# Another order of the work at the boundaries between matrix products: ScalarE norms the first token tile, and the second one's transposes stand inside the third one's tail

## The chip, the cores and the metric

The kernel runs on one core of a Trainium2 chip. The core has a matrix engine (TensorE, PE in the profile), three engines for elementwise work (VectorE or DVE, ScalarE or ACT, GpSimd or POOL), and SyncE (SP), which issues most of the transfers here. Each engine works through its own instructions in order; semaphores make one wait for another. The metric is the device time of one execution in microseconds (us), as a median of runs.

## The reference

One inference step of a backbone with two layers, width 1024, over 384 tokens: 128 of a context pass and 256 latent ones. Both groups use the same weights, but are modulated by different vectors. Everything is float32. Per layer:

```python
def trunk_layer(x, mod, lp, cache):
    sh1, sc1, g1, sh2, sc2, g2 = jnp.split(mod, 6, axis=-1)
    h = rmsnorm(x, lp['g_norm'][0]) * (1.0 + sc1) + sh1
    m, ctx_tensors = token_mixer(h, lp, cache)
    x = x + g1 * rmsnorm(m, lp['g_norm'][1])
    h = rmsnorm(x, lp['g_norm'][2]) * (1.0 + sc2) + sh2
    f = jnp.square(jax.nn.relu(h @ lp['w_mlp1'])) @ lp['w_mlp2']
    x = x + g2 * rmsnorm(f, lp['g_norm'][3])
    return x, ctx_tensors
```

`token_mixer` projects h with `w_in`, runs four branches (retention, S5, gated linear attention, neighbourhood attention), gates their outputs and multiplies the sum by `w_out`. `mod` is a product of `silu(c)` with the weight `w_ada`.

## The kernel before

A product of two float32 matrices is made of three products of parts: each operand is split into a high part (cast to fp32r) and a low part (the rest), and TensorE adds high x high, high x low and low x high in PSUM (the lines L209, L210 and L211 of the profile, in this order). The activations' parts are `hh` and `hl`. The weights come as raw tiles `wf` of 128 x 1024 by DMA; ScalarE casts one to its high part `wh` (L144), VectorE subtracts for the low part `wl` (L156). `prefetch(n)` does this until n weights are ready. Most split weights lie in tiles called `wh` and `wl`, some in spare rows (`rC`, `rB`) or in a spare pair called `r`.

The tokens are three tiles of 128: tile 0 is the context, tiles 1 and 2 are latent. Two kinds of product alternate. In one (`gemm_rows`, `rows`) the tokens are on the output's partitions: a weight row of 128 x 1024 is added into six accumulators of 128 x 512, two a tile. In the other (`gemm_a`, `up`) the output's channels are on the partitions, 128 x 384 each, 24 matmuls.

A layer's residual and norm need whole rows of the accumulators, and the next product needs the normed activations transposed. The function `boundary` orders the work at that place. It is called four times: behind `w_out` in layer 0 (boundary 1, whose tile 1 is transposed at 480.81 us in the trace), behind the MLP of layer 0 (boundary 2, at 775.62), behind `w_out` in layer 1 (boundary 3, at 1210.64), and at the end, with no norm. Inside it the code's order is each engine's order:

- `tail(i, half)`: the last five weight rows, 15 matmuls of 512 columns, for one half of token tile i.
- `residual(i)`, a generator that runs up to its next `yield` at each `next`: ScalarE squares the accumulator (L783), VectorE multiplies it by the gain (L786), VectorE and GpSimd make the reciprocal root (`rstd`, L684 and L685), VectorE updates x (L789), ScalarE squares the new x (L791), a second rstd, and `m` = x times rstd: one half on ScalarE (L797), one on VectorE (L798).
- `normed(i)`: eight transposes of `m` on TensorE (L770) into two PSUM tiles of four channel blocks each. The first four blocks: multiply by the scale and add the shift on VectorE (L812, L813), cast to `hh` on ScalarE (L814). The other four: four calls of 128 columns on ScalarE (L817), the cast on VectorE (L819). VectorE makes both low parts (L818, L820).
- `split`: the first four column blocks ("banks" here) of the next product, each eight matmul triples deep. Over tokens 0 to 255 (tiles 0 and 1) first, 96 matmuls of 256 columns, and then, when tile 2 is normed, over tokens 256 to 383, 96 of 128 columns.

After boundaries 1 and 3, which stand ahead of an MLP, the program goes on with `up(4)`, then in turns one weight row of the second MLP product and one more `up`. Beside it runs a background job, `ada`, for the next modulation vectors: SyncE loads a row block of `w_ada` into a tile `r` (L581), and VectorE multiplies it twice (L583). The tiles `r` come from the same three buffers as the spare weights of the split, so such a load waits until the matmuls that read the spare weight are done.

## Time and profile before

| | |
|---|---|
| median of 3 runs | 1502.18 us (1501.23 to 1503.28) |
| the profiled execution | 1499.83 us, its span 1498.1 us, mean granted clock 0.968 |
| TensorE (PE) | 1418.7 us busy, 95% of the span |
| weight loads (PEld) | 1258.7 us, 84%, beside the matmuls |
| VectorE (DVE) | 938.4 us, 63% |
| ScalarE (ACT) | 653.7 us, 44% |
| GpSimd (POOL) | 338.2 us, 23% |

Busy time is the time in which an engine has an instruction running. The granted clock is TensorE's: 1.00 is its full speed. A matmul's span is longer than its distance to the next one, since matmuls overlap in the array; what counts is the distance between starts.

### The profile page before, as it was taken

The page shows a single profiled execution, that of the slowest core. Times are in us where ns is not written, and L with a number is a line of the kernel's source. Part 1 is how long each engine was busy: PE and PEld are TensorE (multiplying, and loading weights), DVE is VectorE, ACT ScalarE, POOL GpSimd, SP SyncE. Part 2 cuts the span into 40 slices and gives each one's busy share as a digit, 9 for nine tenths or more (in the row PEclk, how much of TensorE's full clock was granted, in tenths as well). Part 3 has the DMA queues.
Part 4 walks back from the last instruction along what each step waited for, and adds up shares of the span by engine and source line. Part 5 has one row for each costly group of instructions (what it writes and reads, how often), then busy time and mean ns, then how long its engine had stood idle before and what let it go on. Part 6 is the DMA issues. An engine that isn't in the chain of part 4 may idle for free. (4 is left out here: it accounts for less than half of the span.)

```text
span 1498.1 us, 22353 instructions
## 1 busy us (share of the span) xinstructions
PE 1418.7 (95%) x8492; PEld 1258.7 (84%) x8492; DVE 938.4 (63%) x1495; ACT 653.7 (44%) x1214; POOL 338.2 (23%) x654
## 2 busy tenths in 40 slices
PE   6989998998997999999989999899899989999998
PEld 5857877898995988888979888688799778999996
DVE  5499941899465867776363577359974658333334
ACT  3446552432334544443453646443233345444443
POOL 5973491011120213320021008500110200000000
PEclk9989997998999999999999999899999999999999
DMA  9545422676334465666445333146653516433342
GB/s 380 158 130 186 132 85 60 197 252 212 127 128 153 151 207 182 203 220 207 139 155 167 110 121 124 49 145 223 209 185 127 193 57 226 140 126 127 126 155 84
DMA packets 93627, 238.16 MB, mean 159 GB/s; under 512 B 17968, under 2 KB 39504, under 8 KB 93520
## 3 DMA queue, kind: packets, MB, share of 16 engines
q1 hardware_dynamic: 90656, 227.75, 46.0%
q0 software_dynamic: 2864, 8.98, 1.9%
q8 instruction: 67, 1.10, 0.3%
q14 instruction: 40, 0.33, 0.1%
HBM read 221.72 MB, written 14.97 MB: 158 GB/s over the span
## 5 line engine op out<-in xcount | busy, mean ns | idle before, releaser
L156 DVE TENSOR_TENSOR wl<-wf,wh 128x1024 fp32r<-128x1024 f32 x257 | 323.5, 1261 | 285.1 <-ACT wh L144 283.9
L144 ACT CAST wh<-wf 128x1024 fp32r<-128x1024 f32 x257 | 268.3, 1046 | 468.3 <-PE mm L210 171.5
L209 PE MATMUL mm<-hh,wh 128*128 128x384 f32 (+3 forms) x808 | 272.5, 337 | 4.4 <-DVE c L1398 3.1
L210 PE MATMUL mm<-hl,wh 128*128 128x384 f32 (+3 forms) x808 | 271.9, 337 | 0.0
L211 PE MATMUL mm<-hh,wl 128*128 128x384 f32 (+3 forms) x808 | 271.7, 336 | 0.0
L211 PE MATMUL mx<-hh,wl 128*128 128x384 f32 (+2 forms) x496 | 164.0, 331 | 1.4 <-DVE wl L156 1.4
L209 PE MATMUL mx<-hh,wh 128*128 128x384 f32 (+2 forms) x496 | 164.6, 332 | 0.0
L210 PE MATMUL mx<-hl,wh 128*128 128x384 f32 (+2 forms) x496 | 163.8, 330 | 0.0
L209 PEld LDWEIGHTS mm<-hh,wh 128*128 128x128 f32 (+1 forms) x808 | 153.1, 190 | 10.4 <-issue 3.6
L210 PEld LDWEIGHTS mm<-hl,wh 128*128 128x128 f32 (+1 forms) x808 | 153.1, 190 | 8.3 <-issue 6.6
L211 PEld LDWEIGHTS mm<-hh,wl 128*128 128x128 f32 (+1 forms) x808 | 152.9, 189 | 5.0 <-issue 2.8
L583 DVE SCALAR_TENSOR_TENSOR mid<-r,fa 128x1024 f32<-128x1024 f32 x80 | 101.6, 1270 | 20.7 <-DMA s_vt<-mid 9.6
L583 DVE SCALAR_TENSOR_TENSOR mid<-r,fb 128x1024 f32<-128x1024 f32 x80 | 100.2, 1252 | 0.2
L209 PEld LDWEIGHTS mx<-hh,wh 128*128 128x128 f32 x496 | 93.3, 188 | 2.9 <-issue 1.0
L211 PEld LDWEIGHTS mx<-hh,wl 128*128 128x128 f32 x496 | 93.3, 188 | 2.5 <-DVE wl L156 2.2
L210 PEld LDWEIGHTS mx<-hl,wh 128*128 128x128 f32 x496 | 93.3, 188 | 1.8
L210 PE MATMUL mm<-wl,rA 128*128 128x512 f32 x216 | 86.6, 401 | 0.0
L209 PE MATMUL mm<-wh,rA 128*128 128x512 f32 x216 | 79.8, 402 | 0.9 <-ACT rA L122 0.7
L211 PE MATMUL mm<-wh,rB 128*128 128x512 f32 x180 | 70.6, 392 | 0.0
L685 POOL TENSOR_TENSOR few<-few,negh 128x1 f32<-128x1 f32 x24 | 13.3, 553 | 221.3 <-DVE few L684 215.0
L700 POOL DMA_DIRECT2D gain<-g x4 | 2.2, 553 | 251.9 <-ACT g L699 231.9
L122 ACT CAST rA<-c 128x384 fp32r<-128x384 f32 x80 | 41.1, 513 | 41.1 <-DVE c L1402 39.3
(505 smaller groups left out, 2836.6 us busy)
## 6 DMA issues: line engine op xcount, KB each, us to landing
wf<-w_mlp SPq DMA_DIRECT2D x128, 512.0 KB, 3.4
r<-w_ada SPq DMA_DIRECT2D x82, 512.0 KB, 3.8
wf<-w_merge SPq DMA_DIRECT2D x64, 512.0 KB, 3.5
wf<-w_in SPq DMA_DIRECT2D x43, 512.0 KB, 3.7
wf<-w_branch SPq DMA_DIRECT2D x16, 512.0 KB, 4.0
wf<-w_out SPq DMA_DIRECT2D x16, 512.0 KB, 3.3
s_vt<-mid SPq DMA_DIRECT2D x16, 256.0 KB, 3.0
mid<-s_vt SPq DMA_DIRECT2D x8, 512.0 KB, 5.7
```

Of the source, the lines that this page charges most:

```text
L122: self.nc.scalar.copy(hi, src)
L144: self.nc.scalar.copy(wh[:, :cols], raw)
L156: self.nc.vector.tensor_tensor(wl[:, :cols], raw, wh[:, :cols].bitcast(F32), op=SUB)
L209: mm(out, lh, rh, start=start, stop=False)
L210: mm(out, lh, rl, start=False, stop=False)
L211: mm(out, ll, rh, start=False, stop=stop)
L583: nc.vector.scalar_tensor_tensor(self.mid([128, D]), w, 0.5, self.cb[g], op0=MUL, op1=MUL, accum_out=mod[:, n, g:g + 1])
L685: self.nc.gpsimd.tensor_tensor(r, v, self.negh[:, 0:1], op=ALU.pow)
L700: nc.gpsimd.dma_start(d[l, which].rearrange("g (k f) -> (g k) f", f=128), rows)
```

## The change

Only `boundary`, `residual`, `normed` and `gemm_rows` change:

- Tile 0 is normed on ScalarE alone (four calls for each of the two transposed tiles); all casts to `hh` are on ScalarE, all subtractions on VectorE.
- Tile 1's eight transposes stand in the middle of tile 2's tail, ahead of its last two weight rows, and not behind it.
- In the split, the matmuls that read `hh` come first within a group and those that read `hl` last; groups are banks 0 and 1 over blocks 0 to 3, then 4 to 7, then bank 2, then tile 2's transposes, then bank 3.
- The second weight of the split goes into two tiles `mid`; all squares write one shared tile of 128 x 512; `residual` has one more `yield`, ahead of its second rstd.
- The first `gemm_rows` of a product runs over the token tiles 2, 1, 0.

```diff
@@ -260,7 +260,7 @@
     def gemm_rows(self, acc, x, start):
 
         w = self.next_w()
-        for i in range(3):
+        for i in (2, 1, 0) if start else range(3):
             for half in range(2):
                 self.rows(acc, i, half, x, w, start, False)
 
@@ -271,55 +271,77 @@
         self.extra += [(room[i], room[i + 1]) for i in range(0, len(room), 2)]
         self.prefetch(TAIL)
         w = [self.loaded.pop(0) for _ in range(TAIL)]
+        junk = self.mid([128, 512])
         if norm:
-            self.extra.append(self.spare_w())
-
-        def tail(i, half):
-            for n in range(TAIL):
+            self.extra += [self.spare_w(), [self.mid([128, 1024], F32R) for _ in range(2)]]
+
+        def tail(i, half, ns=range(TAIL)):
+            for n in ns:
                 self.rows(acc, i, half, xs[n], w[n], False, n == TAIL - 1)
 
-        def split(ps, b, cs, ks):
-            wh, wl = self.loaded[b]
-            for k in ks:
-                ws = slice(k * 128, (k + 1) * 128)
-                self.mm3(ps[:, cs], wh[:, ws], wl[:, ws], self.hh[:, k, cs], self.hl[:, k, cs], k == 0, k == KT - 1)
+        def split(bs, cs, ks):
+            for low in range(2):
+                for b in bs:
+                    wh, wl = self.loaded[b]
+                    for k in ks:
+                        ws = slice(k * 128, (k + 1) * 128)
+                        o, xh, xl = ps[b][:, cs], self.hh[:, k, cs], self.hl[:, k, cs]
+                        if low:
+                            self.nc.tensor.matmul(o, wh[:, ws], xl, start=False, stop=k == KT - 1)
+                        else:
+                            self.nc.tensor.matmul(o, wh[:, ws], xh, start=k == 0, stop=False)
+                            self.nc.tensor.matmul(o, wl[:, ws], xh, start=False, stop=False)
+
+        def do(steps, n=1):
+            for _ in range(n):
+                next(steps)
 
         with self.in_order(), self.first():
-            R = [residual(i) for i in range(3)]
-            N = [self.normed(i, norm) for i in range(3)] if norm else None
-            for i in range(3):
-                for half in range(2):
-                    tail(i, half)
-                if not norm:
+            R = [residual(i, junk) for i in range(3)]
+            if not norm:
+                for i in range(3):
+                    for half in range(2):
+                        tail(i, half)
                     for _ in R[i]:
                         pass
-                    continue
-                if i == 0:
-                    next(R[0])
-                    self.prefetch(1)
-                    next(R[0]), next(R[0])
-                if i == 1:
-                    next(N[0])
-            if not norm:
                 return None
-            next(R[1]), next(R[1]), next(N[0]), next(R[1]), next(N[0])
-            next(N[1])
-            next(N[1]), next(R[2]), next(N[1])
-            self.prefetch(2)
-            next(R[2])
+            N = [self.normed(i, norm) for i in range(3)]
+            tail(0, 0), tail(0, 1)
+            do(R[0])
+            self.prefetch(1)
+            do(R[0], 3)
+            tail(1, 0), tail(1, 1)
+            do(N[0])
+            do(R[1])
+            do(N[0])
+            do(R[1])
+            do(N[0])
+            do(R[1])
+            self.high()
+            do(R[1])
+            self.low()
+            do(N[0])
+            tail(2, 0), tail(2, 1, range(3))
+            do(N[1])
+            tail(2, 1, range(3, TAIL))
+            do(N[1])
+            do(N[0])
+            do(N[1], 4)
+            do(R[2])
+            ps = [self.mmps(), self.mmps(), self.mmps(), self.xps()[:, 0:T]]
+            a, b, lo, hi = slice(0, 256), slice(256, T), range(4), range(4, KT)
+            split((0, 1), a, lo)
+            split((0, 1), a, hi)
             self.prefetch(3)
-            next(R[2])
+            do(R[2])
+            split((2,), a, range(KT))
+            do(R[2], 2)
             self.prefetch(4)
-            ps = [self.mmps(), self.mmps(), self.mmps(), self.xps()[:, 0:T]]
-            a, b = slice(0, 256), slice(256, T)
-            for n in range(4):
-                if n == 3:
-                    next(N[2])
-                split(ps[n], n, a, range(KT))
-            next(N[2]), next(N[2])
-            for ks in (range(4), range(4, KT)):
-                for n in range(4):
-                    split(ps[n], n, b, ks)
+            do(N[2])
+            split((3,), a, range(KT))
+            do(N[2], 4)
+            for ks in (lo, hi):
+                split(range(4), b, ks)
         del self.loaded[0:4]
         for _ in ps:
             self.step()
@@ -770,17 +792,17 @@
...
         halves = slice(0, 512), slice(512, D)
         for h, hs in enumerate(halves):
-            A.activation(junk[:, hs], acc[h], AF.Square, scale=scale * D ** -0.5, accum_out=s[:, h:h + 1])
+            A.activation(junk, acc[h], AF.Square, scale=scale * D ** -0.5, accum_out=s[:, h:h + 1])
             if h:
                 r = self.rstd(s[:, 0:1], s[:, 1:2])
             V.tensor_tensor(m[:, hs], acc[h], gain[:, g, hs], op=MUL)
...
-        u = [self.g3(sh) for _ in range(2)]
-        h = [[t[:, 4 * q:4 * q + 4, cs] for t in (self.hh, self.hl)] for q in range(2)]
-        V.tensor_tensor(u[0], ps[0], scale[:, 0:4].to_broadcast(sh), op=MUL)
-        V.tensor_tensor(u[0], u[0], shift[:, 0:4].to_broadcast(sh), op=ADD)
-        A.copy(h[0][0], u[0])
-        yield
-        for j in range(4):
-            A.activation(u[1][:, j], ps[1][:, j], AF.Identity, scale=scale[:, 4 + j], bias=shift[:, 4 + j])
-        V.tensor_tensor(h[0][1], u[0], h[0][0].bitcast(F32), op=SUB)
-        V.tensor_copy(h[1][0], u[1])
-        V.tensor_tensor(h[1][1], u[1], h[1][0].bitcast(F32), op=SUB)
-        yield
+        for q in range(2):
+            ks = slice(4 * q, 4 * q + 4)
+            u, h = self.g3(sh), self.hh[:, ks, cs]
+            if i and not q:
+                V.tensor_tensor(u, ps[q], scale[:, ks].to_broadcast(sh), op=MUL)
+                V.tensor_tensor(u, u, shift[:, ks].to_broadcast(sh), op=ADD)
+                if i == 1:
+                    yield
+            else:
+                for j in range(4):
+                    A.activation(u[:, j], ps[q][:, j], AF.Identity, scale=scale[:, 4 * q + j], bias=shift[:, 4 * q + j])
+            A.copy(h, u)
+            yield
+            V.tensor_tensor(self.hl[:, ks, cs], u, h.bitcast(F32), op=SUB)
+            yield
```

On TensorE, in boundary 1, around the end of tile 2's tail. `my` is tile 2's second accumulator, `mx` are the transposed tiles, and the rows at L209 on `mm` begin the split. Before:

```order
L211 MATMUL my_4595<-rC_4589,rD_3605 128x512
L209 MATMUL my_4595<-rC_4589,rA_3604 128x512
L210 MATMUL my_4595<-rB_4585,rA_3604 128x512
L211 MATMUL my_4595<-rC_4589,rD_3605 128x512
L209 MATMUL my_4595<-wh_4693,rA_3604 128x512
L210 MATMUL my_4595<-wl_4694,rA_3604 128x512
L211 MATMUL my_4595<-wh_4693,rD_3605 128x512
L770 MATMUL mx_4857<-ident_76,rE_4588 128x128 x4
L770 MATMUL mx_4862<-ident_76,rE_4588 128x128 x4
L209 MATMUL mm_4917<-hh_4683,r_906_4699 128x256
L210 MATMUL mm_4917<-hl_4684,r_906_4699 128x256
L211 MATMUL mm_4917<-hh_4683,r_907_4700 128x256
```

And of the change, from the same matmul on:

```order
L211 MATMUL my_4595<-rC_4589,rD_3605 128x512
L792 MATMUL mx_4857<-ident_76,rE_4588 128x128 x4
L792 MATMUL mx_4862<-ident_76,rE_4588 128x128 x4
L209 MATMUL my_4595<-rC_4589,rA_3604 128x512
L210 MATMUL my_4595<-rB_4585,rA_3604 128x512
L211 MATMUL my_4595<-rC_4589,rD_3605 128x512
L209 MATMUL my_4595<-wh_4693,rA_3604 128x512
L210 MATMUL my_4595<-wl_4694,rA_3604 128x512
L211 MATMUL my_4595<-wh_4693,rD_3605 128x512
L292 MATMUL mm_4895<-hh_4683,r_907_4700 128x256
L293 MATMUL mm_4895<-hh_4683,r_908_4701 128x256
L292 MATMUL mm_4895<-hh_4683,r_907_4700 128x256
```

The two groups of transposes have moved ahead of the last six matmuls of the tail (L770 is now L792), and the split begins with matmuls that read `hh` alone (L292, L293).

On ScalarE, in boundary 1, from tile 1's squares (`few<-mm`, `few<-mx`) on. Before:

```order
L783 ACTIVATE mid_4826,few_4825<-mm_4592 128x512
L783 ACTIVATE mid_4826,few_4825<-mx_4593 128x512
L791 ACTIVATE mid_4826,few_4825<-rX_4574 128x512 x2
L814 CAST hh_4683<-g_923_4843 128x4x128
L797 ACTIVATE rE_4588<-rX_4574,few_4840 128x512
L817 ACTIVATE g_924_4844<-mx_4790,mod_82,ma_898_4681 128x128 x4
L814 CAST hh_4683<-g_927_4867 128x4x128
L783 ACTIVATE mid_4873,few_4872<-my_4594 128x512
L783 ACTIVATE mid_4873,few_4872<-my_4595 128x512
L817 ACTIVATE g_928_4868<-mx_4862,mod_82,ma_898_4681 128x128 x4
L144 CAST wh_4889<-wf_4691 128x1024
```

And of the change, in whose lines L783 is L805, L791 is L813, L797 is L821, L817 is L845 and L814 is L846:

```order
L805 ACTIVATE mid_4699,few_4797<-mm_4592 128x512
L805 ACTIVATE mid_4699,few_4797<-mx_4593 128x512
L845 ACTIVATE g_922_4806<-mx_4787,mod_82,ma_898_4681 128x128 x4
L846 CAST hh_4683<-g_922_4806 128x4x128
L813 ACTIVATE mid_4699,few_4797<-rX_4574 128x512 x2
L144 CAST mid_4702<-wf_4691 128x1024
L821 ACTIVATE rE_4588<-rX_4574,few_4818 128x512
L845 ACTIVATE g_926_4827<-mx_4792,mod_82,ma_898_4681 128x128 x4
L846 CAST hh_4683<-g_926_4827 128x4x128
L846 CAST hh_4683<-g_929_4873 128x4x128
L845 ACTIVATE g_930_4879<-mx_4862,mod_82,ma_898_4681 128x128 x4
L846 CAST hh_4683<-g_930_4879 128x4x128
```

Tile 0's first four calls (`g_922`) and their cast stand between the two pairs of tile 1's squares, a weight's cast into `mid` stands ahead of tile 1's `m`, and tile 2's squares (the next row, of `my`) are behind the casts of tile 1.

On VectorE, in boundary 3, from tile 2's multiply to the `ada` job behind the split. Before:

```order
L812 TENSOR_TENSOR g_2177_11769<-mx_11735,ma_2125_11423 128x512
L813 TENSOR_TENSOR g_2177_11769<-g_2177_11769,mod_85 128x512
L818 TENSOR_TENSOR hl_11426<-g_2177_11769,hh_11425 128x4x128
L819 CAST hh_11425<-g_2178_11770 128x4x128
L820 TENSOR_TENSOR hl_11426<-g_2178_11770,hh_11425 128x4x128
L123 TENSOR_TENSOR rB_11879<-c_2183_11881,rA_11878 128x384
L583 SCALAR_TENSOR_TENSOR mid_11967,mod_85<-r_2211_11965,fa_9839 128x1024
L583 SCALAR_TENSOR_TENSOR mid_11969,mod_85<-r_2211_11965,fb_9840 128x1024
L156 TENSOR_TENSOR wl_11906<-wf_11635,wh_11905 128x1024
```

And of the change (L583 is L605, L812 and L813 are L839 and L840):

```order
L839 TENSOR_TENSOR g_2171_11769<-mx_11735,ma_2121_11423 128x512
L156 TENSOR_TENSOR wl_11906<-wf_11567,wh_11905 128x1024
L840 TENSOR_TENSOR g_2171_11769<-g_2171_11769,mod_85 128x512
L848 TENSOR_TENSOR hl_11426<-g_2171_11769,hh_11425 128x4x128
L848 TENSOR_TENSOR hl_11426<-g_2172_11774,hh_11425 128x4x128
L605 SCALAR_TENSOR_TENSOR mid_11967,mod_85<-r_2205_11965,fa_9839 128x1024
L605 SCALAR_TENSOR_TENSOR mid_11969,mod_85<-r_2205_11965,fb_9840 128x1024
L156 TENSOR_TENSOR wl_11912<-wf_11693,wh_11911 128x1024
```

The cast is gone. The low part of `up(4)`'s weight (`wl_11906`, L156), which stood behind two products of the `ada` job, now stands between multiply and add of tile 2, and the next weight's (`wl_11912`), of the first `gemm_rows`, stands behind those two products.

## Rows read from the trace of the kernel before

**Rows 1.** Waits of TensorE by what ended them: us, times, longest.
```profile
PE mm L209 <- ACT hh L814: 8.1, 3, 2.7
PE mm L210 <- DVE hl L818: 6.4, 3, 2.2
```

**Rows 2.** Windows of boundaries 1 to 3, then 1's last 96 matmuls: length, busy, clock, DMA, GB/s.
```profile
480.81:511.12 30.31, 25.43 (x209) 24.99 (x208) 21.41 (x33) 14.97 (x32) 9.13 (x11) 0.94 0.25 82
775.62:807.15 31.53, 26.60 (x209) 26.16 (x208) 15.51 (x23) 14.00 (x29) 7.46 (x13) 0.89 0.47 155
1210.64:1241.24 30.60, 25.91 (x209) 25.38 (x208) 15.25 (x24) 14.39 (x31) 1.10 (x2) 0.89 0.26 86
500.45:511.12 10.67, 10.67 (x98) 10.67 (x97) 7.56 (x13) 4.76 (x10) 5.19 (x6) 1.00 0.25 84
```

**Rows 3.** Timeline of TensorE in boundary 1: start, length, line, out<-in, [idle before it].
```profile
479.42 0.39 PE L209 MATMUL my<-rC,rA 128*128 128x512 f32 x1
...
480.81 1.04 PE L770 MATMUL mx<-ident,rE 128*128 128x128 f32 x8
...
484.53 0.38 PE L209 MATMUL mm<-hh,r 128*128 128x256 f32 x1 [2.69 <-ACT hh L814]
...
491.31 0.28 PE L209 MATMUL mm<-hh,wh 128*128 128x256 f32 x1
...
496.75 1.03 PE L770 MATMUL mx<-ident,rE 128*128 128x128 f32 x8
```

**Rows 4.** Timeline of boundary 1 on ScalarE, GpSimd and VectorE.
```profile
472.77 0.58 ACT L783 ACTIVATE mid<-mm 128x512 f32<-128x512 f32 x1
...
475.72 0.63 ACT L791 ACTIVATE mid<-rX 128x512 f32<-128x512 f32 x1 [1.71 <-issue]
...
479.20 0.72 ACT L797 ACTIVATE rE<-rX,few 128x512 f32<-128x512 f32 x1
...
479.83 1.48 ACT L817 ACTIVATE g<-mx,mod,ma 128x128 f32<-128x128 f32 x4
...
483.86 0.62 ACT L814 CAST hh<-g 128x512 fp32r<-128x512 f32 x1 [2.55 <-DVE g L813]
...
486.90 1.07 ACT L144 CAST wh<-wf 128x1024 fp32r<-128x1024 f32 x1
...
477.46 0.55 POOL L685 TENSOR_TENSOR few<-few,negh 128x1 f32<-128x1 f32 x1 [2.60 <-DVE few L684]
...
483.13 0.69 DVE L813 TENSOR_TENSOR g<-g,mod 128x512 f32<-128x512 f32 x1
...
488.14 1.22 DVE L156 TENSOR_TENSOR wl<-wf,wh 128x1024 fp32r<-128x1024 f32 x1
...
489.28 1.41 DVE L789 SCALAR_TENSOR_TENSOR rX<-rE,few,rX 128x512 f32<-128x512 f32 x2
```

**Rows 5.** Timeline behind boundary 1's split: the `ada` load on SyncE, its product on VectorE.
```profile
507.18 0.81 SPq L581 DMA_DIRECT2D r<-w_ada  x2
...
511.38 1.23 DVE L583 SCALAR_TENSOR_TENSOR mid<-r,fa 128x1024 f32<-128x1024 f32 x1 [1.25 <-DMA r<-w_ada]
```

**Rows 6.** Windows from the split's end, boundaries 1 and 3, to the second next product's end.
```profile
511.12:524.62 13.50, 13.03 (x68) 11.63 (x68) 13.24 (x19) 8.52 (x15) 0.00 (x0) 1.00 0.75 243
1241.24:1255.09 13.85, 12.77 (x69) 11.67 (x69) 13.85 (x22) 7.77 (x15) 0.00 (x0) 1.00 0.68 223
```

**Rows 7.** All loads of line L581 (`r` from `w_ada`): from issue to landing.
```profile
DMA to landing us min/median/max: 3.0/3.7/5.3
```

**Rows 8.** Timeline of TensorE at two single waits elsewhere.
```profile
334.52 0.44 PE L209 MATMUL mm<-rE,wh 128*128 128x384 f32 x1 [2.17 <-DVE c L1398]
...
457.26 0.49 PE L209 MATMUL mm<-rC,rA 128*128 128x512 f32 x1 [2.55 <-ACT rC L144]
```

**Rows 9.** Windows of TensorE behind these waits; the granted clock follows the busy time.
```profile
458.52:461.92 3.40, 3.16 (x8) 0.65 0.71 195
334.52:337.92 3.40, 3.38 (x18) 1.00 0.66 247
```

More of the change, by code (lines that the diff above doesn't have):

```diff
@@ L771, in transposed, with residual @@
         return ps
-    def residual(self, i, acc, scale, gain, more):
+    def residual(self, i, acc, scale, gain, more, junk):
         nc = self.nc
@@ L779, in residual @@
         s = self.few(4)
-        x, m, junk = self.x[:, i], self.m[:, i], self.mid([128, D])
+        x, m = self.x[:, i], self.m[:, i]
         halves = slice(0, 512), slice(512, D)
         for h, hs in enumerate(halves):
-            A.activation(junk[:, hs], acc[h], AF.Square, scale=scale * D ** -0.5, accum_out=s[:, h:h + 1])
+            A.activation(junk, acc[h], AF.Square, scale=scale * D ** -0.5, accum_out=s[:, h:h + 1])
             if h:
@@ L790, in residual @@
             if more:
-                A.activation(junk[:, hs], x[:, hs], AF.Square, scale=D ** -0.5, accum_out=s[:, 2 + h:3 + h])
+                A.activation(junk, x[:, hs], AF.Square, scale=D ** -0.5, accum_out=s[:, 2 + h:3 + h])
             else:
                 nc.sync.dma_start(self.d["o_x"][i][:, hs], x[:, hs])
-        if more:
-            r = self.rstd(s[:, 2:3], s[:, 3:4])
-            yield
-            A.activation(m[:, halves[0]], x[:, halves[0]], AF.Copy, scale=r)
-            V.tensor_scalar(m[:, halves[1]], x[:, halves[1]], r, None, op0=MUL)
+        if not more:
+            return
+        yield
+        r = self.rstd(s[:, 2:3], s[:, 3:4])
+        yield
+        A.activation(m[:, halves[0]], x[:, halves[0]], AF.Copy, scale=r)
+        V.tensor_scalar(m[:, halves[1]], x[:, halves[1]], r, None, op0=MUL)
         yield
@@ L809, in normed @@
         sh = [128, 4, 128]
-        u = [self.g3(sh) for _ in range(2)]
-        h = [[t[:, 4 * q:4 * q + 4, cs] for t in (self.hh, self.hl)] for q in range(2)]
-        V.tensor_tensor(u[0], ps[0], scale[:, 0:4].to_broadcast(sh), op=MUL)
-        V.tensor_tensor(u[0], u[0], shift[:, 0:4].to_broadcast(sh), op=ADD)
-        A.copy(h[0][0], u[0])
-        yield
-        for j in range(4):
-            A.activation(u[1][:, j], ps[1][:, j], AF.Identity, scale=scale[:, 4 + j], bias=shift[:, 4 + j])
-        V.tensor_tensor(h[0][1], u[0], h[0][0].bitcast(F32), op=SUB)
-        V.tensor_copy(h[1][0], u[1])
-        V.tensor_tensor(h[1][1], u[1], h[1][0].bitcast(F32), op=SUB)
-        yield
+        for q in range(2):
[10 more added lines that the diff above has]
+            A.copy(h, u)
+            yield
+            V.tensor_tensor(self.hl[:, ks, cs], u, h.bitcast(F32), op=SUB)
+            yield
     def h_pairs(self):
@@ L1459, in out_proj @@
         return hs, self.boundary(acc, mg[KT - TAIL:], (r[:, 0], r[:, 1], r[:, 2], r0),
-                                 lambda i: self.residual(i, acc[i], 0.5, gain, True), norm)
+                                 lambda i, junk: self.residual(i, acc[i], 0.5, gain, True, junk), norm)
     def mlp(self, l, hs, first, norm):
@@ L1494, in mlp @@
         return hs, self.boundary(acc, hid[NH - TAIL:], (r[:, 0], r[:, 1], r[:, 2], r0),
-                                 lambda i: self.residual(i, acc[i], 1.0, gain, norm), norm)
+                                 lambda i, junk: self.residual(i, acc[i], 1.0, gain, norm, junk), norm)
     def norm(self, l, part):
```

## The prediction

> **What bounds the kernel now.** TensorE works for nearly the whole span (the table above), so time is lost only where it waits or runs at half clock. I read the waits of the whole span by what ended them, then the three boundaries in windows, then boundary 1 row by row. Two entries of the waits belong to the boundaries: three waits for the cast to `hh`, 8.1 us together, and three for the subtraction to `hl`, 6.4 [rows 1]. The windows run from tile 1's transposes to the first matmul behind the split: 30.31, 31.53 and 30.60 us [rows 2]. The work in one, at full clock: 48 matmuls of 256 columns lie between 491.31 and 496.75, 0.113 each [rows 3], so 96 take 10.9; 10.67 for the 96 of 128 columns, 0.111 each [rows 2]; 16 transposes at the same 0.111, 1.8. That is 23.3, so 7.0, 8.2 and 7.3 us are lost, 22.5 in all: the ceiling. The named waits are 14.5 of it; most of the other 8.0 goes with the granted clock, 0.94, 0.89 and 0.89 in these windows, where the two levels are 1.2 and 2.4 GHz.
>
> In boundary 1 the rows show why. TensorE begins tile 1's transposes at 480.81 and has nothing behind them: multiply and add on VectorE, the cast on ScalarE at 483.86, first matmul at 484.53 after 2.69 us [rows 3, 4]. Its second matmul needs `hl`, which stands on VectorE behind tile 2's work.
>
> **The transposes inside the tail.** Before, 30 matmuls at 0.232 (six from 479.42 to 480.81) stand ahead of the transposes [rows 3]; now 24 do and 6 come behind. ScalarE must have tile 1's `m` ready at 479.4. I chain durations of [rows 4] from the square at 472.77. Two squares of the accumulator now share one junk tile, so the second starts after the first's end, about 0.13 later than before: ScalarE is free at 474.05. New in this place are tile 0's four Identity calls (priced by the row of four, 1.48) and a cast, 0.62: 476.19. Two squares of x, each 0.63, some 0.1 to read its sum and the next one's wait, until 477.59; VectorE's and GpSimd's small steps of the rstd, some 0.85 with the 0.55 of the latter, until 478.43; the second weight's cast, 1.07, fits into that wait. The half `m` (0.72) is done at 479.19. TensorE gets there at 479.36: a margin of 0.17, so the transposes cost no wait. The tail ends at 479.36 + 0.89 + 6 x 0.23 = 481.63. On VectorE multiply and add (0.69 each) follow the first four transposes and end at 481.39. Before, the add that began at 483.13 ended at 483.82 and the matmul came 0.71 later; so now 482.10. **Wait 0.47** where 2.69 stood. The lows-last order removes the 2.20: the first `hl` is wanted 16 matmuls in, its subtraction is done at 482.8.
>
> On the Identity calls the trace prices ScalarE at 1.48 for four and VectorE at 0.69 each for multiply and add, 1.38 [rows 4]. The Trainium skill, page "ScalarE: Activation LUTs", section "Rules for kernel authors", says add and mul belong on VectorE, not ScalarE; that speaks against this edit. Here ScalarE is only 0.10 dearer by those rows, and VectorE's queue is the one that holds `hl` up; by the rule left as before, VectorE's 1.38 would stand ahead of tile 1's add.
>
> **Inside the split.** 48 matmuls of banks 0 and 1 run to 487.6, bank 2's 24 to 490.3. Then come tile 2's transposes, one bank earlier than before. Their chain: ScalarE casts tile 1's two halves first, squares tile 2 from 484.0 to 485.4, casts the third weight to 486.3; its low (1.22) stands on VectorE ahead of the x update (1.41), which so ends at 488.85; squares of x 489.74, rstd 490.58, `m` 491.34 [rows 4]. **Wait 1.08.** Transposes to 492.28; the fourth weight's cast ends at 492.29 (**0.06**), its low at 493.55, and the bank's second matmul wants it (**1.15**). The fifth weight's low then stands between tile 2's multiply and add, so `hh` comes at 496.57 (**0.40**). With 10.67 for the last 96 the split ends at 507.28, not 511.12. Lost in all 3.16. Boundaries 2 and 3 have the same order, so I take 3.16 there too: gains of 3.8, 5.0 and 4.1, 12.9.
>
> **Behind the split.** The bank 0 matmuls end 36 before the split's end now in before, and about 12 in the changed kernel; `w_ada` is loaded into the weight buffers that they release. SyncE issued it at 507.18, 3.9 us before the split's end, and VectorE's `L583` ran at 511.38: 4.2 from issue to use [rows 5]. Now the issue comes about 1.1 us before the end, at 506.2, and the multiply at 510.45. Two of them (1.14 apart) stand on VectorE ahead of a weight's low, done at 513.95. TensorE finishes the next GEMM, 24 matmuls of 384 columns at 0.17 (0.113 x 384 / 256), at 511.4 and can run one or two of what follows: with the lows after it about 2.6 us idle, in boundaries 1 and 3 (2 has no such load). Before, the stretch to the end of the second next GEMM, 48 such matmuls and 18 of 512 columns, some 12.4, took 13.50 and 13.85 [rows 6]: 1.1 and 1.4 lost. New cost 1.5 + 1.2 = 2.7. Bounds: with a landing of 3.0, the shortest of this load, it is 2.4 less; with 5.3, the longest, 2.2 more [rows 7].
>
> **The clock.** After a wait of 2.55, at 457.26, the granted clock was 0.65 on average over 458.52 to 461.92, so the lower level for most of it; after a wait of 2.17, at 334.52, it stayed 1.00 [rows 8, 9]. The new pairs (1.08 and 1.15, 2.2 together, with 0.95 of work between; about 1.5 and 0.9, 2.4 together, behind the split) lie between these two. There are five such places, three in the splits and two behind. A fall costs at least nothing and at most 2.7, the 8.0 above over three boundaries; I take 2.0, since part of that 8.0 is small start gaps. I count one fall.
>
> The Trainium skill, page "TensorE: Matmul & The Clock Gate", section "What's actually happening", calls the throttled state the default, which activity lifts. The trace agrees in direction only (0.65 after a wait of 2.55, 1.00 after 2.17); by the rule alone each of the five could fall, which is the third rival.
>
> **The rest.** gemm_rows in the order 2, 1, 0 after a boundary, the cast to `hh` moved from VectorE to ScalarE and the `mid` pair for the second weight I cost at nothing: the first is followed by the same matmuls, the second is inside the chain above, the third is taken when tile 1's chain allows. What lay in `mid` before loads later, under the 10.67 of the last matmuls, which are ready by then; without that cover a load of 3.0 to 5.3 [rows 7] (the nearest) would show. Between nothing and 0.2 a boundary.
>
> **Sum.** 12.9 - 2.7 = 10.2. The same chaining, done on the rows of before, puts the first matmul at 484.2 where the trace has 484.53; 0.3 off for each boundary: 9.3. One fall: 7.3. Against the profiled execution 1499.83 gives 1492.5; the median of the runs is 2.35 above that execution, so 1502.18 - 7.3 = **1494.9**.
>
> **Rivals.**
> *Shorter waits.* No fall, and the load lands in 3.0: 7.3 + 2.0 + 2.4 = 11.7, 1490.5; without the 0.9, 1489.6. For it: a wait of 2.17 left the clock up. Against: the third weight's low stands ahead of the x update in VectorE's order, whatever the load does.
> *Three falls.* 9.3 - 6.0 = 3.3: 1498.9. For it: a pair behind the split comes close to the 2.55. Against: each pair has work inside.
> *Four or five falls: no gain.* 9.3 - 8.0 or 10.0: 1500.9 to 1502.9, no change that can be measured (0.2%, 3.0 us, is about what a measurement of this kernel can tell). That is also what is left if the lost time only moves behind the split.
> *Slower.* Tile 1's transposes stand in TensorE's order ahead of six tail matmuls that need nothing. If `m` of tile 1 is late, the tail stands too. Its chain has four Identity calls and a cast more ahead of it, and the weight's cast, which waits for a `mid` pair; the margin is 0.17. Each us beyond it costs one per boundary, three in all: 7.3 / 3 = 2.4 us late is no gain, 3.4 (10.3 / 3, with the 3.0 of 0.2%) is slower by 0.2%, about 1505. Against: before, where the cast to `hh` stands ahead of the half `m`, that starts at 479.20 [rows 4], 0.73 later than in my chain; as late as that it would cost 0.6 a boundary.
>
> **Chances.** One or two falls (1494.9 to 1496.9; own range 1493 to 1498): 45%. Shorter waits or no fall (below 1493): 25%. Three: 14%. No gain: 10%. Slower: 6%. Faster by over 0.2% needs under 1499.2: 45 + 25 + 14 = 84%; within 0.2% 10%; slower 6%. The range is 1489 to 1499: it leaves out the 16 above, and a few of the 25 below.
>
> **What would show it.** Windows of 26 to 28 us over the boundaries in place of 30 to 31; under 0.8 us waited at the split's first matmul and no wait for `hl` there; about 1.1 before tile 2's transposes and 1.1 for a weight's low at bank 3; `r<-w_ada` issued within 1.5 us of the split's end and a wait for a low of more than 1.5 behind it in boundaries 1 and 3; the clock at 0.50 in one or two of these stretches. Wrong if tile 1's transposes wait inside the tail, if the waits of `hh` are still above 1.5, or if the clock is down at every boundary.

## The result, and the profile after

The changed kernel takes 1485.09 us (median of 4 runs, 1480.47 to 1492.61) against 1501.83 for the kernel before beside it (1501.23 to 1503.28): a ratio of 0.9891, 95% interval 0.9861 to 0.9921, 16.7 us less. Forecast were 7.3 us less and 1489 to 1499. Ratios and intervals, here and below, leave out a run that is over 1.5% above the fastest of its kernel; there is one such, named where it stands. The profiled execution took 1480.47 us, 19.4 less than that of before; the differences below are between these two.

The sections of the page after, first the span and the busy times of each engine:

```profile
span 1478.7 us, 22371 instructions
...
PE 1408.7 (95%) x8492; PEld 1247.2 (84%) x8492; DVE 929.9 (63%) x1480; ACT 665.4 (45%) x1235; POOL 337.4 (23%) x654
```

The shares don't tell the two kernels apart: TensorE is at 95% in both. The waits of TensorE by what ended them do (us in total, times, longest):

```profile
PE mx L792 <- ACT rE L821: 2.7, 3, 1.0
...
PE mx L293 <- DVE wl L156: 2.6, 3, 0.9
...
PE mm L292 <- ACT hh L846: 1.1, 3, 0.4
```

These answer to [rows 1]. The 8.1 us for `hh` are 1.1, the 6.4 for `hl` are gone, and two waits foretold have come: for tile 2's `m` (0.9 each) and for the fourth weight's low (0.87 each). The windows, first of the three boundaries and then of what follows boundaries 1 and 3 (length, busy time of PE, PEld, DVE, ACT, POOL, granted clock, DMA share, GB/s):

```profile
480.35:509.76 29.41, 27.22 (x216) 26.14 (x215) 19.30 (x31) 15.38 (x33) 8.49 (x11) 0.94 0.37 118
772.00:800.20 28.20, 26.06 (x215) 24.77 (x215) 13.68 (x20) 14.60 (x31) 6.72 (x13) 1.00 0.52 166
1195.10:1223.25 28.15, 26.05 (x216) 24.75 (x215) 14.40 (x21) 14.52 (x32) 1.10 (x2) 1.00 0.31 96
509.76:523.56 13.80, 13.80 (x74) 12.85 (x74) 13.75 (x21) 9.85 (x18) 0.00 (x0) 1.00 0.71 238
1223.25:1237.42 14.17, 14.17 (x76) 13.22 (x76) 14.17 (x24) 9.81 (x18) 0.00 (x0) 1.00 0.78 256
```

They answer to [rows 2] and [rows 6]. The first three hold six matmuls of the tail more than before, 6 x 0.232 = 1.39. Without these they are 28.0, 26.8 and 26.8 against 30.3, 31.5 and 30.6: gains of 2.3, 4.7 and 3.8, 10.8 in all. The column to look at is the clock: 1.00 in boundaries 2 and 3, where it was 0.89, and 0.94 in boundary 1, as before, where it fell once. In the last two rows TensorE is busy from edge to edge; before, these stretches lost 1.1 and 1.4, so another 2.5 came back where 2.7 were to be lost.

13.3 of 19.4 are found. The rest lies far from any line of the diff, in layer 1's S5 branch, in matmuls of mostly 96 and 48 columns behind a wait of 3.6 us. The windows of TensorE from that wait's end, first before and then after (length, busy, clock, DMA share, GB/s):

```profile
962.54:976.22 13.68, 13.68 (x56) 0.50 0.32 84
976.22:978.50 2.28, 2.28 (x8) 0.53 0.59 196
```

```profile
955.63:964.42 8.79, 8.79 (x56) 0.81 0.18 41
964.42:978.50 14.08, 14.08 (x115) 1.00 0.43 131
```

The same 56 instructions take 13.68 us and 8.79, and about 1.1 more follows at half clock before: 6 us. So 10.8 + 2.5 + 6 = 19.3. The sum closes because two smaller differences cancel: TensorE comes to boundary 1 some 0.9 us later than before, and some 1.3 are gained between the S5 branch and boundary 3.

### The profile page after: what moved, and what is told of

It is laid out like the page before. It is cut to its first block, busy times and chain, and to the rows that moved or that the text cites. A ratio compares the mean times of both kernels' runs of the same rounds, so it can differ in the third digit from the quotient of the medians.

```text
span 1478.7 us, 22371 instructions
## 1 busy us (share of the span) xinstructions
PE 1408.7 (95%) x8492; PEld 1247.2 (84%) x8492; DVE 929.9 (63%) x1480; ACT 665.4 (45%) x1235; POOL 337.4 (23%) x654
## 5 line engine op out<-in xcount | busy, mean ns | idle before, releaser
L156 DVE TENSOR_TENSOR wl<-wf,wh 128x1024 fp32r<-128x1024 f32 (+1 forms) x254 | 319.8, 1261 | 284.9 <-ACT wh L144 284.6
L144 ACT CAST wh<-wf 128x1024 fp32r<-128x1024 f32 (+1 forms) x254 | 264.6, 1045 | 456.5 <-PE mm L210 171.3
L209 PE MATMUL mm<-hh,wh 128*128 128x384 f32 (+1 forms) x712 | 244.4, 343 | 5.7 <-DVE c L1426 4.3
L211 PE MATMUL mm<-hh,wl 128*128 128x384 f32 (+1 forms) x712 | 244.5, 343 | 0.0
L210 PE MATMUL mm<-hl,wh 128*128 128x384 f32 (+1 forms) x712 | 244.4, 343 | 0.0
L209 PE MATMUL mx<-hh,wh 128*128 128x384 f32 x448 | 151.1, 337 | 0.0
L211 PE MATMUL mx<-hh,wl 128*128 128x384 f32 x448 | 150.5, 336 | 0.0
L210 PE MATMUL mx<-hl,wh 128*128 128x384 f32 x448 | 150.4, 336 | 0.0
L209 PEld LDWEIGHTS mm<-hh,wh 128*128 128x128 f32 (+1 forms) x712 | 133.9, 188 | 11.8 <-issue 4.5
L210 PEld LDWEIGHTS mm<-hl,wh 128*128 128x128 f32 (+1 forms) x712 | 133.9, 188 | 8.1 <-issue 6.2
L605 DVE SCALAR_TENSOR_TENSOR mid<-r,fa 128x1024 f32<-128x1024 f32 x80 | 101.6, 1271 | 30.1 <-DMA r<-w_ada 13.4
L605 DVE SCALAR_TENSOR_TENSOR mid<-r,fb 128x1024 f32<-128x1024 f32 x80 | 100.2, 1252 | 0.2
L209 PEld LDWEIGHTS mx<-hh,wh 128*128 128x128 f32 x448 | 84.2, 188 | 2.8 <-issue 1.0
L209 PE MATMUL mm<-wh,rA 128*128 128x512 f32 x216 | 79.7, 400 | 0.7 <-ACT rA L122 0.7
L707 POOL TENSOR_TENSOR few<-few,negh 128x1 f32<-128x1 f32 x24 | 13.3, 555 | 219.0 <-DVE few L706 211.9
```

The lines of the kernel that those rows point to most:

```text
L144: self.nc.scalar.copy(wh[:, :cols], raw)
L156: self.nc.vector.tensor_tensor(wl[:, :cols], raw, wh[:, :cols].bitcast(F32), op=SUB)
L209: mm(out, lh, rh, start=start, stop=False)
L210: mm(out, lh, rl, start=False, stop=False)
L211: mm(out, ll, rh, start=False, stop=stop)
L605: nc.vector.scalar_tensor_tensor(self.mid([128, D]), w, 0.5, self.cb[g], op0=MUL, op1=MUL, accum_out=mod[:, n, g:g + 1])
```

## The experiments

For each run of a kernel there are a span and a mean granted clock. Span times clock is about the span as if at full clock, called the full-clock span here: it holds what TensorE does and waits, and the clock holds the rest. The kernel before has 1450.4 (mean of 53 runs) at a mean clock of 0.9665; the changed one 1442.9 at 0.9725 (12 runs): 7.5 us of work and waits, and 1443 x (1/0.9665 - 1/0.9725) = 9.2 us of clock. The full-clock span is the steadier measure: these runs lie within 5 us of their kernel's mean, while the times of one kernel spread over up to 16. What a fall of the clock costs besides is in the time. Each experiment's kernel ran beside the kernel before; the ratios to that one are what is compared.

**Transposes behind the tail.**

```diff
-            tail(2, 0), tail(2, 1, range(3))
+            tail(2, 0), tail(2, 1)
             do(N[1])
-            tail(2, 1, range(3, TAIL))
             do(N[1])
```

> The changed kernel (1485.1 us) with one part undone: tile 1's transposes stand behind all 30 matmuls of tile 2's tail again. Theory: the moved transposes cover the norm of tile 1 with six matmuls, 1.4 us, and nothing else of the gain hangs on them. TensorE then waits 0.34 + 1.4 = 1.7 us at the first matmul of each split, three times, 4.2 us more in all, and a wait of that length beside the 0.9 and 0.9 further on lets the clock fall at one or two boundaries more, 1.3 to 1.7 each: 1489 to 1493. Rival: the order of the split (lows last) carries the gain and the place of the transposes nothing: 1485, within 1 us.

Measured: 1489.86 us, ratio 0.9909 (0.9887 to 0.9930), full-clock span 1448.2. TensorE in boundary 1, from its timeline (the same in boundaries 2 and 3, 1.73 and 1.72):

```profile
486.86 0.38 PE L292 MATMUL mm<-hh,r 128*128 128x256 f32 x1 [1.73 <-ACT hh L845]
```

The wait is 1.3 to 1.4 longer, as six matmuls are worth, three times; the full-clock span grows by 5.3. In the time the interval overlaps that of the changed kernel, so the 4 us show in the waits and the full-clock span, not by the median alone.

**Products side by side in the split.**

```diff
-            for low in range(2):
-                for b in bs:
...
+            for b in bs:
+                wh, wl = self.loaded[b]
+                for k in ks:
+                    ws = slice(k * 128, (k + 1) * 128)
+                    self.mm3(ps[b][:, cs], wh[:, ws], wl[:, ws], self.hh[:, k, cs], self.hl[:, k, cs], k == 0, k == KT - 1)
```

> The changed kernel with the split's groups kept, but each block's three matmuls side by side again (high x high, high x low, low x high). Theory: the low part of tile 1 is done about 0.7 us after its high part, so the second matmul waits 0.7 us three times: 2 us more, 1487; behind the split nothing changes, since the spare weight's two tiles now come free 36 matmuls before the end, both in time. Rival: the lows-last order took away the whole wait of 2.2 us for hl that the kernel before had: 6.6 us more, 1492.

Measured: 1493.40 us, ratio 0.9946 (0.9926 to 0.9967), full-clock span 1446.9, mean clock 0.9695. The time is the rival's, its cause isn't: the waits for `hl` at the split's start are 0.3 each, not 2.2. In its profiled execution the clock fell in boundary 1 at 490.6 us, some 1.8 us into the gapless run of tile 2's matmuls of 128 columns, which had begun behind waits of 0.66 and 0.17. The window from the first of them to just behind the split's end:

```profile
488.05:508.18 20.13, 19.96 (x100) 0.56 0.31 99
```

These are the 96 matmuls that take 10.67 at full clock [rows 2] and a few of 384 columns; at a mean clock of 0.56 some 9 of the 20.13 us are lost, and another 1.4 until the clock came back at 511.0, in the next product of 384 columns. A fall in the changed kernel that came a little earlier, behind 0.99 and 0.87, was over after 3.4 us, ahead of these matmuls:

```profile
495.20:498.60 3.40, 3.40 (x18) 0.52 0.61 208
```

So a fall that comes at the narrow matmuls cost some 10 us here, where 2.0 was taken for one. This is one execution. In the seven other profiles of the changed kernel and its variants (those with the S5 transposes below left aside) no fall inside a split is longer than some 4 us, and all of them have the lows last; that the order is what avoids the long one is likely, not shown.

**The spare weight freed last.**

```diff
-            for ks in (lo, hi):
-                split(range(4), b, ks)
+            split(range(4), b, lo)
+            split((1, 2, 3), b, hi)
+            split((0,), b, hi)
```

> The changed kernel with bank 0 of the split's last group put at the end, so that both tiles of the spare weight come free with the last matmuls of the split and the load of w_ada is issued within 0.5 us of the split's end, not 4.3 us before it. VectorE's order moves with it: the low parts of the next two weights then stand ahead of the ada products. The prediction's step: a late load costs TensorE 2.6 us behind the split in boundaries 1 and 3, or 5 us and more with the clock: 1490 to 1494. Theory now: the load was early in the changed kernel, and where it is late the products stand behind the low parts and hold up nobody: 1485, within 1 us, and no wait of TensorE over 0.5 us behind the split.

Measured: 1487.08 us, ratio 0.9893 (0.9873 to 0.9912), full-clock span 1443.9, as the changed kernel. The timeline of SyncE and VectorE behind the split, whose end is at 509.36:

```profile
509.11 0.82 SPq L604 DMA_DIRECT2D r<-w_ada  x2
...
508.86 2.36 DVE L156 TENSOR_TENSOR wl<-wf,wh 128x1024 fp32r<-128x1024 f32 x2 [2.95 <-ACT wh L144]
512.88 1.23 DVE L606 SCALAR_TENSOR_TENSOR mid<-r,fa 128x1024 f32<-128x1024 f32 x1 [1.66 <-DMA r<-w_ada]
```

The load is issued 0.25 us before the end and used 3.8 later, as foretold for a late load; but both lows now stand ahead of the `ada` product, and TensorE waits for nothing there. So a late load costs nothing by itself where the lows stand ahead of it. What it costs with the `ada` products held ahead of the lows, as the prediction had it, was not run.

**Lows last alone, in the kernel before.**

```diff
-            for k in ks:
-                self.mm3(...)
+            for low in range(2):
+                for k in ks:
...
```

> The kernel before (1501.8 us) with one part of the change alone: in the split, the matmuls that read hl come last within each bank; the transposes stay behind the tail and the norm stays as it was. Theory: the wait of 2.2 us for hl only turns into one for the second half of hh, whose cast stands on VectorE behind tile 2's work and ends 2.1 us after the first matmul is due to pass it: waits as before, 1500 to 1503. Rival: the order alone is worth the 2.2 us three times and one clock fall each: 1490 to 1496.

Measured: 1503.54 us, ratio 1.0001 (0.9991 to 1.0011). The wait for `hl` became one for the cast of the second half of `hh`, 0.9 to 1.5 us, and the 2.69 stayed; in boundary 1:

```profile
485.56 0.58 PE L289 MATMUL mm<-hh,r 128*128 128x256 f32 x1 [2.69 <-ACT hh L819]
488.59 0.58 PE L289 MATMUL mm<-hh,r 128*128 128x256 f32 x1 [0.94 <-DVE hh L824]
```

By itself the order gives nothing.

**The S5 wait filled**, in the kernel before and in the changed one:

```diff
             ps = self.yps()
+            if pp == 0:
+                self.tc.cur_priority += 5000
+                for _ in range(28):
+                    nc.tensor.transpose(ps[:, 0:128], self.ident, self.ident)
+                self.tc.cur_priority -= 5000
```

> The kernel before with one thing added in both layers: 28 transposes of the identity matrix, 3.1 us of needless work for TensorE, in the wait ahead of the S5 branch's small matmuls (96 and 48 columns), so that TensorE isn't idle there; their result is overwritten. In the profiled execution of before the 17 us behind that wait were at half clock in layer 1 (7.9 us lost) and in layer 0 (9.7 lost); in the changed kernel's only in layer 0. Theory: the state of the clock in these stretches has nothing to do with the change; with the wait filled they stay at full clock more often in both kernels, and the kernel before gets 5 to 15 us faster than 1503.3, 1488 to 1498. Rival: the added work is not hidden and the clock falls all the same: 1503 to 1509.

> The changed kernel with the same 28 transposes in the same two waits. Theory: of the 16.7 us, some 12 come from the boundaries (7 us of waits, 5 of clock falls in the three splits) and the rest from the chance of the clock in the S5 stretches; with these filled in both kernels the changed one is 10 to 13 us faster than the other one of this pair. Rival: the change itself carries it all: 16 to 18 us between the pair.

Measured: 1495.15 us, ratio 0.9941 (0.9921 to 0.9961), and 1473.42 us (6 runs, 1467.70 to 1490.35), ratio 0.9813 (0.9775 to 0.9851), without the run of 1490.35. In layer 1 the clock stays up in both; the windows there of the kernel before with the transposes, and of the changed one:

```profile
969.00:985.00 16.00, 16.00 (x121) 1.00 0.36 107
```

```profile
950.00:975.00 25.00, 25.00 (x191) 1.00 0.48 124
```

With the wait of 3.6 us down to 0.9 and 0.26, the clock didn't fall there in either profile. The 28 needless transposes are worth 8 us before and 12 us after (9 when the run of 1490.35 is counted). They also moved six other matmuls of this stretch behind the narrow ones, so that the wait alone is the cause is likely, not isolated. In layer 0 they ran too early: a wait of 2.9 us was left, and the clock fell behind it in both. The pair is 1.28% apart, give or take 0.43%: 19 us, 13 to 26 (17 when that run is counted). That is more than the 10 to 13 of the theory and leaves room for the rival's 16 to 18. The full-clock spans of all runs differ by 7.5 (1453.6 and 1446.1), just as without the transposes; the rest is clock (0.9742 and 0.9805), and part of it is layer 0's S5 stretch, ahead of every boundary: 0.51 in 235 to 256 in the one profile, 0.83 in 231 to 250 in the other. The changed kernel with the transposes is the fastest of all by its median, and its interval lies below that of the changed one; when that run is counted, the two overlap.

**Tile 0's first half on VectorE.**

```diff
-            if i and not q:
+            if not q:
```

> The changed kernel with tile 0's first four blocks scaled and shifted on VectorE again (two instructions of 0.69 us in place of four calls of 1.5 us together on ScalarE). Theory: ScalarE is free 1.5 us earlier ahead of tile 1's squares of x, VectorE has 1.4 us more in the same place; the chain to tile 1's m runs through both, so it ends within 0.5 us of where it was, and the transposes inside the tail wait at most 0.5 us: 1485 to 1487. Rival: norming tile 0 on ScalarE is what gets m ready in time, and each boundary loses 1 to 1.5 us: 1488 to 1490.

Measured: 1492.13 us, ratio 0.9931 (0.9915 to 0.9946), full-clock span 1447.1. Tile 1's transposes now wait inside the tail:

```profile
483.44 1.09 PE L792 MATMUL mx<-ident,rE 128*128 128x128 f32 x8 [0.63 <-ACT rE L821]
```

Here 0.63, then 0.68 and 0.63: between theory and rival, 1.9 us in all, though the time lies above both ranges; the full-clock span grows by 4.2, so 2.3 of it aren't found in these waits. The rest of the 7 us is clock: in this profile layer 1's S5 stretch was at half, as before. On VectorE the multiply and add, 0.69 each, stand ahead of tile 1's update of x, which `m` needs. The Trainium skill, "ScalarE: Activation LUTs", "Rules for kernel authors", sends add and mul to VectorE, as this version does; here that costs 0.6 us a boundary.

**Without the pair of mid tiles.**

```diff
-            self.extra += [self.spare_w(), [self.mid([128, 1024], F32R) for _ in range(2)]]
+            self.extra.append(self.spare_w())
```

> The changed kernel without the pair of mid tiles: the second weight of the split goes into an ordinary wh and wl pair again. The order of the instructions stays as it is in the split. Theory: with one pair fewer, up(4)'s weight can be cast only when a pair comes free in the split, and its low part is late behind it, as it was before: 1 to 1.5 us more in boundaries 1 and 3, 1487 to 1489. Rival: nothing waits for a pair, 1485, within 1 us.

Measured: 1498.32 us (12 runs), ratio 0.9973 (0.9954 to 0.9993), full-clock span 1452.4: all of the 7.5 us are gone, and 2 more, beyond what either theory or rival had. TensorE behind the splits of boundaries 1 and 3, and VectorE behind the first:

```profile
511.41 0.69 PE L211 MATMUL mx<-hh,wl 128*128 128x384 f32 x1 [2.01 <-DVE wl L156]
...
1237.87 0.69 PE L211 MATMUL mx<-hh,wl 128*128 128x384 f32 x1 [1.64 <-DVE wl L156]
```

```profile
507.72 1.23 DVE L605 SCALAR_TENSOR_TENSOR mid<-r,fa 128x1024 f32<-128x1024 f32 x1 [2.63 <-DMA r<-w_ada]
...
508.99 1.22 DVE L605 SCALAR_TENSOR_TENSOR mid<-r,fb 128x1024 f32<-128x1024 f32 x1
...
510.14 1.22 DVE L156 TENSOR_TENSOR wl<-wf,wh 128x1024 fp32r<-128x1024 f32 x1
```

This is a wait of the prediction's kind, `ada` products ahead of a low that TensorE wants, but for another weight: without the pair it is the low of `up(4)` itself, wanted at once. Its high part is waited for as well, 0.31 and 0.24 just ahead. Behind boundary 2 it is 1.1 for the high part and 0.65 for the low. With 0.38 inside each tail and 0.5 more at bank 3 that makes 7.6 us of waits, and the clock fell behind all three splits.

**The pair alone, in the kernel before.**

```diff
-            self.extra.append(self.spare_w())
+            self.extra += [self.spare_w(), [self.mid([128, 1024], F32R) for _ in range(2)]]
...
-        x, m, junk = self.x[:, i], self.m[:, i], self.mid([128, D])
+        x, m = self.x[:, i], self.m[:, i]
```

> The kernel before with one part of the change alone: the second weight of the split goes into a pair of mid tiles, and all squares share one tile. So up(4)'s weight is split inside the boundary, as in the changed kernel; transposes, norms and the order of the split stay as they were. Theory: the pair takes the waits behind the splits, 1.1 and 1.4 us in boundaries 1 and 3, and leaves the 2.7 and 2.2 in front; 2.5 us less, and no more than one clock fall: 1499 to 1501. Rival: as the changed kernel loses 13 us without the pair, the pair is worth as much here: 1490.

Measured: 1501.22 us (12 runs), ratio 0.9994 (0.9972 to 1.0016), full-clock span 1448.1, 2.3 less. That is the theory's size: nothing waits behind the splits, and in front TensorE waits as before, here in boundary 1:

```profile
485.93 0.38 PE L209 MATMUL mm<-hh,r 128*128 128x256 f32 x1 [2.92 <-ACT hh L815]
488.63 0.58 PE L210 MATMUL mm<-hl,r 128*128 128x256 f32 x1 [2.32 <-DVE hl L819]
```

**Token tiles 0, 1, 2 behind the split, and the changed kernel again.**

```diff
-        for i in (2, 1, 0) if start else range(3):
+        for i in range(3):
```

> The changed kernel with the first weight row after a boundary run over the token tiles 0, 1, 2 again. Theory: nothing waits there by more than 0.3 us, so no change: 1485, as the changed kernel beside it, within 3 us. Rival: the order 2, 1, 0 is what keeps TensorE from waiting behind the split (2.6 us were foretold there): 5 us more.

> The changed kernel itself, on the chip of the two others of this call, since it had four runs only and they spread over 12 us. Theory: the waits at the boundaries are as in its first profile (0.3, 0.9 and 0.9 us), the time follows the mean granted clock, and the product of span and clock is 1444 us again, against 1451 for the kernel before; median 1484 to 1490. Rival: its first runs were lucky as a whole, 1490 to 1494.

Measured: 1486.47 us, ratio 0.9906 (0.9874 to 0.9937), and 1486.73 us (8 runs, 1476.62 to 1492.34), ratio 0.9898 (0.9863 to 0.9932). The order of the token tiles does nothing that shows, and the changed kernel's first runs weren't lucky as a whole. Its second profile repeats the first one: the same waits, boundary 1 with its fall, and the S5 stretch in layer 1, whose windows are

```profile
955.56:959.28 3.72, 3.70 (x12) 0.54 0.00 0
959.28:974.14 14.86, 14.86 (x117) 1.00 0.39 120
```

## Why the prediction was wrong

**What bounds the kernel** was read rightly for the most part: the three boundaries and what follows them gave back 13.3 of the 19.4 us. Some 6 came from the S5 branch, where the prediction didn't look.

**The transposes inside the tail** held nearly to the tenth. Foretold were no wait inside the tail and 0.47 at the split; measured 0 and 0.34, 0.40 and 0.32. The rows of boundary 1 after, on ScalarE, VectorE and TensorE:

```profile
479.45 0.72 ACT L821 ACTIVATE rE<-rX,few 128x512 f32<-128x512 f32 x1
...
481.71 0.69 DVE L840 TENSOR_TENSOR g<-g,mod 128x512 f32<-128x512 f32 x1
...
482.44 0.62 ACT L846 CAST hh<-g 128x512 fp32r<-128x512 f32 x1 [0.22 <-DVE g L840]
...
480.35 1.04 PE L792 MATMUL mx<-ident,rE 128*128 128x128 f32 x8
...
483.11 0.39 PE L292 MATMUL mm<-hh,r 128*128 128x256 f32 x1 [0.34 <-ACT hh L846]
...
492.55 1.09 PE L792 MATMUL mx<-ident,rE 128*128 128x128 f32 x8 [0.99 <-ACT rE L821]
...
494.74 0.39 PE L293 MATMUL mx<-hh,wl 128*128 128x256 f32 x1 [0.87 <-DVE wl L156]
```

`m`, the add and the cast follow each other as chained from [rows 4], about 1.0 later throughout, as the transposes are (480.35 against the 479.36 foretold). `m` is done at 480.17, 0.18 ahead of the transposes; the margin foretold was 0.17. Undoing the edit brought 1.3 to 1.4 back at each boundary.

**Inside the split** 1.08, 0.06 + 1.15 and 0.40 were foretold; 0.99, 0.87 and nothing over 0.25 were measured in boundary 1 (where the clock had not fallen ahead of it, in three other profiles, the last one is 0.53 to 0.63 there). With the 0.9 taken off and one fall at 2.0 the three splits were to bring 12.9 - 0.9 - 2.0 = 10.0; they brought 10.8.

**Behind the split is the step that failed**: "Now the issue comes about 1.1 us before the end, at 506.2, and the multiply at 510.45." The pair of buffers `r` was taken as freed together, by the last matmul that reads the spare weight. (There are two such buffers, not three as the description above says, and the spare weight holds both.) They come free one by one. The 12 matmuls from the last read to the split's end that the prediction counts are right for the high tile; for the low tile they are 40. The rows behind boundary 1, on TensorE, SyncE and VectorE:

```profile
505.18 0.28 PE L293 MATMUL mm<-hh,r 128*128 128x128 f32 x1
...
507.97 0.61 PE L290 MATMUL mm<-hl,r 128*128 128x128 f32 x4
...
505.49 0.33 SPq L603 DMA_DIRECT2D r<-w_ada  x1
...
509.57 1.23 DVE L605 SCALAR_TENSOR_TENSOR mid<-r,fa 128x1024 f32<-128x1024 f32 x1 [3.52 <-PE mm L290]
...
512.00 1.22 DVE L156 TENSOR_TENSOR wl<-wf,wh 128x1024 fp32r<-128x1024 f32 x1
...
514.20 0.40 PE L210 MATMUL my<-wl,rA 128*128 128x512 f32 x1
```

The lows-last order reads the spare weight's low tile for the last time at 505.18, and 0.31 later the load is issued into it: 4.3 us before the split's end at 509.76, no later than the 3.9 of before. The low part that stands behind both products is done at 513.22, and TensorE wants it at 514.20: a margin of 1.0 where a wait of 2.6 was foretold. (For the multiply the row names a matmul as what ended its wait; the load landed 4.0 us after its issue, at 509.49, so the two came together.) Behind boundary 3 it is the same: issued at 1218.97, 4.3 ahead of the end at 1223.25, and the low part done at 1225.88, while the next weight row begins at 1227.46. So the term was +2.5 instead of -2.7, 5.2 us, more than half of the 9.4 by which the gain was missed. Taken apart, the forecast of 7.3 holds about 6.0 of clock (8.0 less one fall) and 1.3 of waits (12.9 - 8.0 - 0.9 - 2.7); the means of all runs give 9.2 and 7.5. Whether a load issued so late would have cost the 2.6 foretold is not shown; the nearest are the 2.01 and 1.64 us without the `mid` pair, for another weight and with an early load.

That pair was put at nothing in "the rest". It is worth more than the whole gain of waits, 9.5 us of full-clock span against 7.5, since it lets `up(4)`'s weight be split inside the boundary; alone, in the kernel before, it is worth 2.3. The gain belongs to the parts together: the split moved forward only pays if what stands behind it is ready as early.

**The clock.** One fall of five was foretold, and one came in each profile of the changed kernel, in boundary 1, at about the price taken: 0.94 over 29.41 us is 1.8 lost. But the bracket it was read from, 1.00 after a wait of 2.17 and 0.65 after one of 2.55, does not hold: behind the 2.55 a second wait follows, which the prediction left out, on TensorE of the kernel before:

```profile
458.52 0.50 PE L210 MATMUL mm<-rC,rA 128*128 128x512 f32 x1 [0.77 <-DVE rC L156]
```

And falls came behind 0.99 and 0.87, and behind 0.66 and 0.17. The same 0.99 and 0.87 were followed by a fall in boundary 1 of the second profile and by none in boundary 3, so which place falls is open. That fewer fall goes with the change: in the three profiles of the kernel before and its variants without the transposes (before itself, lows last, the pair alone) the clock fell in all nine splits, in the eight of the changed kernel and its variants in 7 of 24.

The Trainium skill, "TensorE: Matmul & The Clock Gate", "What's actually happening", says that "activity releases the throttle", and the prediction weighed it. The trace does not agree for the 96 matmuls of 128 columns above: busy 19.96 of 20.13 us, at a clock of 0.56. Nor did the sum have a price for such a fall, and nothing in it looked outside the boundaries, where layer 1's S5 stretch gave 6 us. That stretch was at half in all three profiles of the kernel before and its variants named above, and short in six of eight of the changed kernel and its variants. Its instructions and the wait ahead, 3.5 to 3.6, are the same in all of them. That the wait bears on it is seen by filling it; why the changed kernel mostly escapes is open.

**The rivals.** "Shorter waits" was the nearest, at 1489.6 to 1490.5 with 25%; neither of its conditions came: there was a fall, and the load landed in 4.0 us, not 3.0. "Three falls", "no gain" and "slower" are excluded by the clock and the waits shown.

## What to carry to other kernels

When an order changes, look up for each buffer which instruction reads it last; two tiles of one pair may come free 28 matmuls apart, and the transfer waiting for the pair starts with the first. Price the parts of a change together: one that takes a wait away in front needs the one that has the next operand ready behind. When a wait on TensorE is priced, a fall of the clock may come on top of its length: in these traces none, 1.8 us or, where 96 matmuls of 128 columns followed, some 10. Look at the clock outside the place that was changed, too: a third of the profiled gain lay there.

## What was not expected of the hardware

In one execution half clock held for 20 us, through almost all of 96 gapless matmuls of 128 columns and into the next product, and in several through 14 us and more of mostly 96 and 48 columns; in the changed kernel it was over after 3.7 us in the midst of these. The changed kernel's runs spread over 12 to 16 us with the mean granted clock (0.968 to 0.977 in the first four, at full-clock spans of 1443.1 to 1444.7), where most runs of the kernel before lie within 7. Filling most of a wait of 3.6 us with 28 needless transposes came with a clock of 1.00 behind it and made both kernels faster, by 0.6% before and 0.8% after (0.6% when the run left out is counted).
